# Weaving the experts of a mixture layer: products of four experts ahead of the down products of the four before

## The chip, the cores and the metric

The kernel runs on one core of a Trainium2 chip. The metric is the device time of one execution in microseconds (us). TensorE is called PE (PEld is its weight load), VectorE DVE, ScalarE ACT, GpSimd POOL, and SyncE SP. POOL and SP issue the transfers (DMAs) of this kernel's last stage.

## The reference, cut to what matters

The model is two blocks on 512 tokens of width 1024. Only the last part of the second block is touched by the change, a mixture of 32 experts in 4 groups, of which each token uses 2. In outline (the names are those of the reference or of the kernel):

```
h2 = rmsnorm(x) * (1 + scale2) + shift2            # 512 x 1024
group = argmax of 4 group logits; the 2 best of its 8 experts, with weights
for each token and each of its two experts e:
    a = silu(h2 @ w_gate[e]) * (h2 @ w_up[e])      # 256 wide
    x += gate2 * weight * (a @ w_down[e])          # 1024 wide
```

All weights are float32. An expert has 1024 x 256 for the gate, the same for up, and 256 x 1024 for down: 3 MB, so 96 MB for the 32 experts, and all of it is fetched from memory once.

## The kernel before, in words

The two blocks' dense products come first; their weights pass through `Stream`, a list of fetches in a fixed order (`order`). A fetch takes a free place of 128 x 2048 floats (1 MB) from `st.slots`, and `st.free` hands the place back when its last product is issued; `st.fill` then starts the next fetch on SP. SP issues in order, so a fetch whose place is not yet read out holds the later ones back. In the last stage there are 13 places: three of `wr`, seven of `wb` and three of `wq`.

Then comes the routing (L1840 to L2041): logits, the two best experts, a place in a table of 8 rounds x 256 rows for each token and expert (`hidx`, `r4s`). `keep_busy(n)` puts n products on PE that nobody reads. `rows_in(q)` gathers the 256 rows of round `q` from memory by two indirect DMAs on POOL into `gb[q % 2]`.

The experts are done in `NQ` = 8 rounds of four. A round fetches 12 places: 8 for gate and up (`gu`, one for each 128 of the 1024 inputs, all four experts side by side) and 4 for down (`dn`). Rows are two tiles: r = 0, in which each expert has its own 32 rows, and r = 1, whose four groups of 32 rows each belong to an expert chosen by the routing. For r = 1 `deal` copies the four 512-wide pieces of the place, chosen by registers, into `wd` (two on DVE, two on ACT; two buffers). `product` makes four 32-row products that run beside each other, and it is called once with the place itself and once with `wd`.

The order of one round is written out by hand and is the same on every engine:

- `turned` transposes and scales the gathered rows: PE products with a diagonal matrix `dg`, and 8 evictions that alternate between ACT and DVE, into `xT`;
- 8 times: `deal`, two `product`s into `bank[0]` and `bank[1]`, `st.free`, `st.fill`;
- `act` (tanh on ACT, two multiplications on DVE) for both tiles;
- `turn(q + 1, r)` for both tiles, with the gather of round q + 2 behind the second;
- `act_T` (PE transposes, ACT copies) for both tiles;
- 4 times: `deal`, two `product`s; `halves` multiplies the results into `yo` on DVE;
- two `scatter`s, indirect DMAs on POOL that add the rows of `yo` to the output in memory. Each waits for the one before it to land, as rows may repeat; only the two of the last round don't wait for each other.

`later` holds small work (`slot_weights`, the weights of the rows, and `crowded`, for experts with more rows than fit), which is stepped after a round, and `slot_weights` stands behind the first place of round 0.

Of the kernel before, what the change touches and what calls it, by code (L numbers as in the profile page):

```python
# [12 lines left out]
FT = mybir.dt.float32  # L13
# [7 lines left out]
D = 1024  # L21
# [19 lines left out]
LOTS = 32 * MAGIC  # L41
MORE0 = 7
Z1 = (1, 0, 0, 1, 2, 2, 2)
# [315 lines left out]
def tile_kernel(ctx: ExitStack, tc: tile.TileContext, ws, ada, c_d, hT_d, cst_d, seq_d, bd_d, wr_d, pos_d, out):  # L359
# [54 lines left out]
    class Stream:  # L414
# [3 lines left out]
        def __init__(self, order):  # L418
            self.order = order
            self.lp = self.sp = self.up = 0  # L420
            self.hold, self.queue = False, nc.sync
            self.raw, self.done, self.used = {}, {}, {}
            self.slots = deque(wpool.tile([128, 2048], FT, name=f"wr{i}") for i in range(self.WR))
            parts = [wpool.tile([128, 2, 1024], FR, name="wp", tag="P", bufs=self.PARTS) for _ in range(self.PARTS)]
            self.parts = deque([t[:, 0], t[:, 1]] for t in parts)

        def more(self, slots, parts):
            self.slots.extend(B([128, 2048], name="wb") for _ in range(slots))
# [47 lines left out]
        def free(self, key):  # L476
            self.slots.append(self.raw.pop(key))

# [51 lines left out]
    n_dense = [name for name, *_ in plan].index("gu")  # L530
    for n in range(len(plan)):
# [1332 lines left out]
    gb = [B([128, 2, D], name="gb") for _ in range(2)]  # L1864
    for g in gb:
        G.memset(g, 0.0)

# [54 lines left out]
    V.tensor_add(cnt_h, oh[:, 0], oh[:, 1])  # L1922
    keep_busy(2)

# [84 lines left out]

    xT = [B([128, 2, 8, 128], name="xT") for _ in range(2)]  # L2010
    wd = [B([128, 4, 512], name="wd") for _ in range(2)]
    yo = B([128, 2, D], name="yo")

# [4 lines left out]
    rows_in(0)  # L2018
    rows_in(1)
    st.hold, st.queue = False, G  # L2020
# [19 lines left out]
    V.tensor_copy(tot, pt)  # L2040
    keep_busy(6)  # L2041

    def slot_weights():

        S.activation(ex, ex, AF.Exp)
        V.reduce_sum(pg, gx, axis=AX.X)
        V.reciprocal(pg, pg)
        V.tensor_scalar(m1, ex, 1.0, None, op0=OP.add)
        V.reciprocal(m1, m1)
        V.tensor_mul(wk[:, :4], pg, m1)  # L2050
        V.tensor_mul(wk[:, 4:], wk[:, :4], ex)
# [3 lines left out]
        inv3 = bank[3][:, 32:64]  # L2055
        by_slot(inv3, ohb, lambda n: tkw[:, n].rearrange("p v a -> p (v a)"))
        values(w_s, inv3)
# [7 lines left out]
    ex_w, ex_j, hidx2 = (cpool.tile([128, NX], I32, name=n) for n in ("ex_w", "ex_j", "hidx2"))  # L2065
    r4s2, w_s2 = (cpool.tile([128, NX], FT, name=n) for n in ("r4s2", "w_s2"))

    def crowded():
# [28 lines left out]
        yield  # L2097
        inv = bank[4][:, :80]
        by_slot(inv, ohb, lambda n: tks[n // 4][:, n % 4].rearrange("p v a -> p (v a)"))
# [19 lines left out]

    def turned(x, g, scale, banks, tag="vm"):  # L2120

        d = mpool.tile([128, 128], FT, name="dg", tag=tag, bufs=1)
        V.tensor_scalar(d, ident, scale, None, op0=OP.mult)  # L2123
        for h, p in enumerate(banks):
# [16 lines left out]

    def act_T(a, p):
        for k in range(2):
            PE.transpose(p[:, 128 * k:128 * k + 128], a[:, 128 * k:128 * k + 128], ident)
        aT = mpool.tile([128, 2, 128], FT, name="aT", tag="fxpm")
        S.copy(aT, p[:, :256].rearrange("p (k s) -> p k s", k=2))
        return aT
# [4 lines left out]

    def turn(q, r):
        turned(xT[q % 2][:, r], gb[q % 2][:, r], r4s[:, 2 * q + r:2 * q + r + 1], bank[4:6] if r else bank[6:8],
               "vfm" if r else "vm")
        if r and q + 2 < NQ:
            rows_in(q + 2)
# [4 lines left out]
    dealt = [0]  # L2162

    def deal(n, regs):

        st.need(("w", n))
        w = st.raw["w", n]
        t = wd[dealt[0] % 2]
        dealt[0] += 1
        for j in range(4):  # L2170
            (V.tensor_copy if j < 2 else S.copy)(t[:, j], w[:, bass.ds(regs[j], 512)])  # L2171
        return w, t
# [7 lines left out]
    def own(w):  # L2180
        return lambda j: w[:, 512 * j:512 * j + 512]

    def done(n):
        st.free(("w", n))
        st.fill()

    st.fill()
    scatters = []
    regs = lot_regs(0)
    first = [deal(n_dense + k, regs) for k in range(2)]  # L2190
    turn(0, 0)
    for q in range(NQ):
        n0 = n_dense + 12 * q
        x = xT[q % 2]
        for k in range(8):
            w, t = first.pop(0) if first else deal(n0 + k, regs)
            for r in range(2):
                if q == k == 0 and r == 1:
                    turn(0, 1)
                product(bank[r], lambda c: x[:, r, k, c], (lambda j: t[:, j]) if r else own(w), k == 0, k == 7)  # L2200
            if q == k == 0:
                slot_weights()
                later.add(crowded())
            done(n0 + k)
        a = [act(bank[r]) for r in range(2)]
        if q + 1 < NQ:
            for r in range(2):
                turn(q + 1, r)
        aT = [act_T(a[r], bank[6 + r]) for r in range(2)]

        def halves(h):
            for r in range(2):
                V.scalar_tensor_tensor(yo[:, r, 512 * h:512 * h + 512], bank[2 + 2 * h + r], w_s[:, 2 * q + r:2 * q + r + 1],
                                       gate[h], op0=OP.mult, op1=OP.mult)

        for h in range(2):
            for k in range(2):
                n = n0 + 8 + 2 * h + k
                w, t = deal(n, regs)
                for r in range(2):  # L2220
                    product(bank[2 + 2 * h + r], lambda c: aT[r][:, k, c], (lambda j: t[:, j]) if r else own(w), k == 0, k == 1)
                done(n)
                if h and not k:
                    halves(0)
        halves(1)
        if q + 1 < NQ:
            regs = lot_regs(q + 1)
        before_q = scatters[-1:]
        scatters = [scatter(yo[:, r], hidx[:, 2 * q + r:2 * q + r + 1]) for r in range(2)]
        if q == NQ - 1:  # L2230

            tc.declare_no_dep(scatters[1].ins, scatters[0].ins, reason="no row of out in both")
            tc.add_manual_dep(scatters[1].ins, before_q[0].ins.name,
                              mybir.DependencyInfo(mybir.DependencyClass.Sync, mybir.DependencyReason.DATA),
                              reason="rows of out added to before")
        later.tick()
        later.tick()
    later.finish()
# [6 lines left out]
    with tc.For_i(0, n_any, 1) as _:  # L2245
        n_x = vload(nx_i[0:1, 0:1], NX)
        with tc.For_i(0, n_x, 1) as i:
# [10 lines left out]
            V.tensor_copy(sw[:, 1:], w_s2[:, bass.ds(i, 1)])  # L2258
            g, x, y = gb[0][:, 0], xT[0][:, 0], yo[:, 1]
            gather(g, idx)  # L2260
            turned(x, g, sw[:, :1], bank[6:8])
# [3 lines left out]
            V.memset(yo[:, 0, :1], 0.0)  # L2265
            for h in range(2):
# [31 lines left out]
```

## Time and profile before

| what | value |
|---|---|
| median of 3 runs | 1641.91 us (1639.06 to 1643.56) |
| the profiled execution, its own time | 1641.11 us |
| its span in the trace | 1639.3 us |
| PE busy, share of the span | 1532.5 us, 93% |
| DVE, ACT, POOL busy | 927.4, 659.1, 200.5 us |
| moved by DMA over the whole span | 258.28 MB, mean 158 GB/s |

The span runs from the first to the last record of the program. The rest of the profiled time, 1.8 us, lies outside it. All times of rows are counted from the span's start. The last stage begins near 1313 us, when the dense products end.

### The profile page before, as it was taken

How to read it: one execution, taken by the hardware profiler on the slowest of the kernel's cores; microseconds unless marked ns; L12 is line 12 of the kernel's file. 1: busy time of each engine (PE TensorE's matmuls, PEld its weight loads, DVE VectorE, ACT ScalarE, POOL GpSimd, SP SyncE). 2: the span in 40 equal slices, each digit the busy share in tenths (PEclk: the TensorE clock that was granted, in tenths of full speed). 3: DMA queues.
4: the chain of work that ended last, by engine and by line, in shares of the span. 5: the costliest groups of instructions: out<-in, count | busy, mean ns of one | idle time of the engine just before them, and what ended most of it. 6: DMA issues, size and time to landing. Idle time of an engine off the chain costs nothing. (4 is left out here: it accounts for less than half of the span.)

```text
span 1639.3 us, 22545 instructions
## 1 busy us (share of the span) xinstructions
PE 1532.5 (93%) x8512; PEld 1173.7 (72%) x8512; DVE 927.4 (57%) x2020; ACT 659.1 (40%) x1208; POOL 200.5 (12%) x255
## 2 busy tenths in 40 slices
PE   7899999999999899999999999999999977877785
PEld 6788777788888678888889887778887843433432
DVE  5655456355667776654445746953666355555453
ACT  4445443326533232222234446543233224544553
POOL 0100111020030300000004223100114030111101
PEclk9999999999999999999999999999999989999998
DMA  5221221122245355454222322123226648999993
GB/s 194 81 78 66 101 68 64 66 105 88 78 176 196 126 208 197 181 189 166 103 78 104 128 91 77 53 78 106 74 78 271 208 158 329 363 382 357 372 384 82
DMA packets 49327, 258.28 MB, mean 158 GB/s; under 512 B 7316, under 2 KB 15636, under 8 KB 21184
## 3 DMA queue, kind: packets, MB, share of 16 engines
q1 hardware_dynamic: 41680, 237.17, 38.2%
q0 software_dynamic: 7248, 19.65, 4.1%
q8 instruction: 67, 1.10, 0.3%
q14 instruction: 44, 0.36, 0.1%
q10 hardware_dynamic: 288, 0.01, 0.0%
HBM read 250.48 MB, written 14.71 MB: 162 GB/s over the span
## 5 line engine op out<-in xcount | busy, mean ns | idle before, releaser
L485 DVE TENSOR_TENSOR wp<-wr,wp 128x1024 fp32r<-128x1024 f32 (+1 forms) x198 | 246.1, 1246 | 198.8 <-ACT wp L484 198.1
L484 ACT CAST wp<-wr 128x1024 fp32r<-128x1024 f32 (+1 forms) x198 | 204.0, 1034 | 110.6 <-PE bank L584 82.2
L582 PE MATMUL bank<-uh,wp 128*128 128x512 f32 (+1 forms) x464 | 150.9, 361 | 5.4 <-DVE ka L789 4.4
L584 PE MATMUL bank<-ul,wp 128*128 128x512 f32 (+1 forms) x464 | 144.5, 348 | 0.0
L586 PE MATMUL bank<-uh,wp 128*128 128x512 f32 (+1 forms) x464 | 144.1, 347 | 0.0
L582 PE MATMUL bank<-fh,wp 128*128 128x512 f32 x304 | 119.4, 393 | 6.6 <-ACT wp L484 6.6
L586 PE MATMUL bank<-fh,wp 128*128 128x512 f32 x304 | 119.3, 392 | 0.6 <-DVE wp L485 0.5
L584 PE MATMUL bank<-fl,wp 128*128 128x512 f32 x304 | 119.1, 392 | 0.2 <-POOL fl L1180 0.2
L582 PE MATMUL bank<-z,wp 128*128 128x512 f32 x264 | 108.4, 411 | 0.0
L586 PE MATMUL bank<-z,wp 128*128 128x512 f32 x264 | 103.2, 391 | 0.0
L584 PE MATMUL bank<-z,wp 128*128 128x512 f32 x264 | 103.0, 390 | 0.0
L2178 PE MATMUL bank<-wd,xT 128*32 128x512 f32 x512 | 87.5, 629 | 13.0 <-DVE wd L2171 13.0
L582 PEld LDWEIGHTS bank<-uh,wp 128*128 128x128 f32 x464 | 81.0, 190 | 24.1 <-issue 6.8
L586 PEld LDWEIGHTS bank<-uh,wp 128*128 128x128 f32 x464 | 81.2, 190 | 11.2
L584 PEld LDWEIGHTS bank<-ul,wp 128*128 128x128 f32 x464 | 81.2, 190 | 9.9
L2171 ACT COPY wd<-wb 128x512 f32 x108 | 60.6, 621 | 55.3 <-PE bank L2178 38.6
L582 PE MATMUL bank<-ah,wp 128*128 128x512 f32 (+1 forms) x218 | 76.1, 349 | 0.0
L584 PE MATMUL bank<-al,wp 128*128 128x512 f32 (+1 forms) x218 | 75.9, 348 | 0.0
L586 PE MATMUL bank<-ah,wp 128*128 128x512 f32 (+1 forms) x218 | 75.9, 348 | 0.0
L582 PEld LDWEIGHTS bank<-fh,wp 128*128 128x128 f32 x304 | 57.6, 189 | 19.3 <-ACT wp L484 7.4
L2126 PE MATMUL bank<-dg,gb 128*128 128x128 f32 x256 | 38.9, 315 | 30.8 <-DVE dg L2123 30.8
L586 PEld LDWEIGHTS bank<-fh,wp 128*128 128x128 f32 x304 | 57.4, 189 | 13.5 <-DVE wp L485 1.7
(629 smaller groups left out, 3263.0 us busy)
## 6 DMA issues: line engine op xcount, KB each, us to landing
wr<-in_ws_dram SPq DMA_DIRECT2D x115, 1024.0 KB, 4.8
wb<-in_ws_dram SPq DMA_DIRECT2D x54, 1024.0 KB, 10.8
wr<-in_ada_dram SPq DMA_DIRECT2D x24, 1024.0 KB, 5.2
wq<-in_ws_dram SPq DMA_DIRECT2D x21, 1024.0 KB, 9.4
wr<-in_ws_dram SPq DMA_DIRECT2D x4, 768.0 KB, 4.2
ncb<-cum_d POOLq DMA_DIRECT2D x8, 264.0 KB, 3.8
wr<-in_ws_dram SPq DMA_DIRECT2D x4, 512.0 KB, 5.6
h_d<-row SPq DMA_DIRECT2D x8, 256.0 KB, 3.9
```

Source lines behind the costliest of these rows:

```text
L484: S.copy(h[:, :fl], t)
L485: eng.tensor_sub(l[:, :fl], t, h[:, :fl].bitcast(FT))
L582: PE.matmul(ps, lhsT=wh(k), rhs=rh(k, sl), start=first and k == 0, stop=False)
L584: PE.matmul(ps, lhsT=wh(k), rhs=rl(k, sl), start=False, stop=False)
L586: PE.matmul(ps, lhsT=wl(k), rhs=rh(k, sl), start=False, stop=last and k == nk - 1)
L2126: PE.matmul(p[:, 128 * t:128 * t + 128], lhsT=g[:, 512 * h + 128 * t:512 * h + 128 * t + 128], rhs=d, start=True, stop=True)
L2171: (V.tensor_copy if j < 2 else S.copy)(t[:, j], w[:, bass.ds(regs[j], 512)])
L2178: PE.matmul(ps[c], lhsT=x(c), rhs=w(j), start=first, stop=last)
```

## The change

The order of the fetches and of all engines' work in the expert stage is changed. The 12 places of a round are no longer worked in one piece: the list `jobs` has the 8 gate and up places of round q, then the 4 down places of round q - 1. One loop over `jobs` does `deal` for the next place, then both products of the present one. What stood between gate/up and down (`act`, `act_T`, `turn`, the gather) is put behind single places of the next round by `beside`: `act` of round q - 1 behind place 0 of round q, `act_T` behind 2, the two `turn`s of round q + 1 behind 4 and 6. Gate and up sums alternate between banks 0, 1 and banks 2, 3; down sums use banks 4 to 7.

`EARLY` = 3 further places are added before the routing, so that 16 places can be fetched ahead. When the first three of the places drawn from pool `B` are freed they are not used for fetches again: they become the second `gb` and `xT` and `yo`. So the gather of round 1 and the zeroing of its `gb` move behind place 2 of round 0. `slot_weights` moves from place 0 to place 2 of round 0, its last part to round 1. `keep_busy` gets 9, 8 and 2 products where it had 2, 5 and 6 (a fourth call keeps its 2).

```diff
-MORE0 = 7
+MORE0, EARLY = 7, 3
...
+    fours = [(q, n_dense + 12 * q) for q in range(NQ)]
+    jobs = []
+    for q, n in fours:
+        jobs += [(q, n + k) for k in range(8)]
+        if q:
+            jobs += [(q - 1, n - 4 + k) for k in range(4)]
+    jobs += [(NQ - 1, n + 8 + k) for k in range(4)]
+    order += [("w", n) for _, n in jobs]
...
         def free(self, key):
-            self.slots.append(self.raw.pop(key))
+            t = self.raw.pop(key)
+            if self.left and any(t is x for x in self.early):
+                self.left -= 1
+                self.early = [x for x in self.early if x is not t]
+            else:
+                self.slots.append(t)
...
+    st.more(EARLY, 0)
     st.fill()
     st.hold = True
...
-    keep_busy(2)
+    keep_busy(9)
...
-    keep_busy(5)
+    keep_busy(8)
...
     rows_in(0)
-    rows_in(1)
...
-    keep_busy(6)
+    keep_busy(2)
...
+    def beside(q, k):
+
+        other = bank[2 - 2 * (q % 2):4 - 2 * (q % 2)]
+        aside[0] = other[1]
+        if q and k == 0:
+            acts(q - 1)
+        elif q and k == 2:
+            acts_T(q - 1)
+        elif k in (4, 6) and q + 1 < NQ:
+            turn(q + 1, k // 2 - 2, other)
+            if k == 6 and q + 2 < NQ:
+                rows_in(q + 2)
+        if q == 0 and k == 2:
+            rows_place()
+            rows_in(1)
+            yo.append(B([128, 2, D], name="yo"))
+            later.add(slot_weights())
+        elif q == 1 and k == 3:
+            later.finish()
+            later.add(crowded())
+        elif q > 1 and k in (5, 7):
+            later.tick()
...
+    for i, (q, n) in enumerate(jobs):
+        if i + 1 < len(jobs):
+            dealt[i + 1] = deal(i + 1)
+        w, t = dealt.pop(i)
+        k = n - n_dense - 12 * q
+        for r in range(2):
...
+            product(ps, x, (lambda j: t[:, j]) if r else own(w), first, last)
+        st.free(("w", n))
+        w = t = None
+        st.fill()
+        if k < 8:
+            beside(q, k)
+        elif k == 10:
+            halves(q, 0)
+        elif k == 11:
+            halves(q, 1)
+            add_rows(q)
+            aT.pop(q)
```

## Rows read from the trace of the kernel before

**Rows 1.** Page, busy tenths of the DMA engines in 40 slices of 41 us.

```profile
DMA  5221221122245355454222322123226648999993
```

**Rows 2.** Windows, one round: us; PE, PEld, DVE, ACT, POOL busy; granted clock; DMA.

```profile
1387.00:1402.00 15.00, 14.77 (x120) 7.15 (x120) 6.04 (x17) 7.22 (x13) 1.56 (x1) 0.89 1.01 378
1402.00:1412.50 10.50, 4.65 (x39) 4.11 (x36) 4.80 (x14) 4.11 (x11) 2.09 (x2) 1.00 0.98 403
1412.50:1420.00 7.50, 7.46 (x64) 2.14 (x64) 5.19 (x12) 5.94 (x12) 0.00 (x0) 1.00 0.74 276
1420.00:1423.00 3.00, 1.00 (x9) 0.96 (x8) 2.24 (x4) 0.85 (x2) 1.62 (x1) 1.00 0.97 311
```

**Rows 3.** Timeline, the same round from its last gate and up products on.

```profile
1400.05 1.20 PE L2178 MATMUL bank<-wb,xT 128*32 128x512 f32 x8
...
1400.91 1.20 PE L2178 MATMUL bank<-wd,xT 128*32 128x512 f32 x8
...
1403.77 2.05 PE L2126 MATMUL bank<-dg,gb 128*128 128x128 f32 x16 [1.66 <-DVE dg L2123]
1404.97 0.46 ACT L2133 ACTIVATE xT<-bank,mod,a 128x128 f32<-128x128 f32 x1 [2.36 <-PE bank L2126]
...
1408.34 2.05 PE L2126 MATMUL bank<-dg,gb 128*128 128x128 f32 x16 [2.52 <-DVE dg L2123]
...
1412.54 1.06 PE L2178 MATMUL bank<-wr,aT 128*32 128x512 f32 x8 [1.71 <-ACT aT L2146]
```

**Rows 4.** DMA queues from 1380 to 1608 us: packets, MB, share of 16 engines.

```profile
DMA packets 13706, 83.47 MB, mean 366 GB/s; under 512 B 2844, under 2 KB 2844, under 8 KB 4216
...
q1 hardware_dynamic: 10666, 77.58, 84.8%
q0 software_dynamic: 3020, 5.63, 10.6%
```

**Rows 5.** Windows, columns as in rows 2: the stretch, fetches alone, after the last fetch.

```profile
1380.00:1608.00 228.00, 180.49 (x1462) 89.38 (x1458) 119.57 (x299) 114.96 (x227) 29.39 (x21) 0.94 0.96 366
...
1400.00:1410.00 10.00, 5.82 (x50) 4.20 (x43) 3.66 (x10) 2.95 (x7) 1.06 (x1) 1.00 1.01 421
...
1608.00:1610.00 2.00, 2.00 (x24) 1.05 (x20) 0.99 (x3) 1.42 (x3) 0.27 (x1) 1.00 0.03 8
```

**Rows 6.** Timeline of SP: the fetches of the last stage as they restart.

```profile
1315.14 1.67 SPq L440 DMA_DIRECT2D wq<-in_ws_dram  x3
...
1351.22 9.93 SPq L440 DMA_DIRECT2D wb<-in_ws_dram  x6
```

**Rows 7.** Timeline of PE and POOL from the routing to the third place.

```profile
1315.07 1.88 PE L1862 MATMUL bank<-mbig,ident 128*128 128x512 f32 x4
1319.97 0.62 PE L1928 MATMUL bank<-cnt,marks 128*128 128x32 f32 x4 [3.02 <-DVE cnt L1922]
...
1327.12 1.35 PE L1987 MATMUL bank<-tk,ohb 128*128 128x16 f32 x8
...
1329.60 1.14 POOL L2006 DMA_INDIRECT gb<-h_d,hidx  x1 [3.29 <-DVE tk L1982]
...
1336.17 1.95 PE L2126 MATMUL bank<-dg,gb 128*128 128x128 f32 x16
...
1349.18 1.94 PE L2178 MATMUL bank<-wb,xT 128*32 128x512 f32 x8
```

**Rows 8.** One line's instructions, the gathers L2006 from 1327 to 1339 us.

```profile
DMA to landing us min/median/max: 4.0/4.3/5.8
```

**Rows 9.** Timeline of POOL at the end: the scatters of the last two rounds.

```profile
1599.88 1.71 POOL L2150 DMA_INDIRECT out_dram<-yo,hidx  x1 [19.93 <-DVE yo L2213]
1609.73 1.67 POOL L2150 DMA_INDIRECT out_dram<-yo,hidx  x1 [8.14 <-DVE wd L2171]
1624.43 1.56 POOL L2150 DMA_INDIRECT out_dram<-yo,hidx  x1 [13.03 <-DVE yo L2213]
```

**Rows 10.** DMA issues from 1608.5 to 1615 us: count, us to landing.

```profile
out_dram<-yo,hidx POOLq DMA_INDIRECT x1, 4.6
```

More of the change, by code (lines that the diff above doesn't have):

```diff
@@ L422, in __init__ @@
             self.raw, self.done, self.used = {}, {}, {}
+            self.early, self.left = [], 0
             self.slots = deque(wpool.tile([128, 2048], FT, name=f"wr{i}") for i in range(self.WR))
@@ L427, in more @@
         def more(self, slots, parts):
-            self.slots.extend(B([128, 2048], name="wb") for _ in range(slots))
+            new = [B([128, 2048], name="wb") for _ in range(slots)]
+            self.slots.extend(new)
+            self.early.extend(new)
             for _ in range(parts):
@@ L530, in tile_kernel @@
     n_dense = [name for name, *_ in plan].index("gu")
-    for n in range(len(plan)):
+    for n in range(n_dense):
         order.append(("w", n))
@@ L1862, in keep_busy, with rows_place @@
             PE.matmul(bank[1], lhsT=ident, rhs=io, start=True, stop=True)
-    gb = [B([128, 2, D], name="gb") for _ in range(2)]
-    for g in gb:
-        G.memset(g, 0.0)
+    gb, xT, yo = [], [], []
+    def rows_place():
+        gb.append(B([128, 2, D], name="gb"))
+        G.memset(gb[-1], 0.0)
+        xT.append(B([128, 2, 8, 128], name="xT"))
+    rows_place()
     sc, used = [], [0]
@@ L2054, in slot_weights @@
         spread_a(G, tkw, tf, tok[:, :, 3:])
-        inv3 = bank[3][:, 32:64]
+        yield
+        inv3 = bank[7][:, :32]
         by_slot(inv3, ohb, lambda n: tkw[:, n].rearrange("p v a -> p (v a)"))
@@ L2117, in crowded, with norm_of, turned @@
             yield
-    def turned(x, g, scale, banks, tag="vm"):
+    def norm_of(scale, tag):
         d = mpool.tile([128, 128], FT, name="dg", tag=tag, bufs=1)
         V.tensor_scalar(d, ident, scale, None, op0=OP.mult)
+        return d
+    def turned(x, g, d, banks):
         for h, p in enumerate(banks):
@@ L2140, in act, with act_T @@
         return a
-    def act_T(a, p):
+    def act_T(a, p, aT=None):
         for k in range(2):
             PE.transpose(p[:, 128 * k:128 * k + 128], a[:, 128 * k:128 * k + 128], ident)
-        aT = mpool.tile([128, 2, 128], FT, name="aT", tag="fxpm")
+        if aT is None:
+            aT = mpool.tile([128, 2, 128], FT, name="aT", tag="fxpm")
         S.copy(aT, p[:, :256].rearrange("p (k s) -> p k s", k=2))
@@ L2151, in scatter, with turn, deal @@
                                     in_offset=None, bounds_check=SEQ - 1, oob_is_err=False, compute_op=OP.add)
[L2153 to L2157, printed above, removed]
+    def turn(q, r, banks):
+        turned(xT[q % 2][:, r], gb[q % 2][:, r], norm_of(r4s[:, 2 * q + r:2 * q + r + 1], "vfm" if r else "vm"), banks)
     def lot_regs(q):
         return [vload(lot_i[0:1, 4 * q + j:4 * q + j + 1], 1536, [ET.DVE if j < 2 else ET.Activation]) for j in range(4)]
-    dealt = [0]
-    def deal(n, regs):
+    regs, dealt = {}, {}
+    def deal(i):
+        q, n = jobs[i]
+        if n == n_dense + 12 * q:
+            regs[q] = lot_regs(q)
         st.need(("w", n))
         w = st.raw["w", n]
-        t = wd[dealt[0] % 2]
-        dealt[0] += 1
+        t = wd[i % 2]
         for j in range(4):
-            (V.tensor_copy if j < 2 else S.copy)(t[:, j], w[:, bass.ds(regs[j], 512)])
+            (V.tensor_copy if j < 2 else S.copy)(t[:, j], w[:, bass.ds(regs[q][j], 512)])
         return w, t
@@ L2181, in own @@
         return lambda j: w[:, 512 * j:512 * j + 512]
[L2183 to L2229, printed above, removed]
@@ L2230, in tile_kernel, with halves, add_rows @@
+    def halves(q, h):
+        for r in range(2):
+            V.scalar_tensor_tensor(yo[0][:, r, 512 * h:512 * h + 512], bank[4 + 2 * h + r], w_s[:, 2 * q + r:2 * q + r + 1],
+                                   gate[h], op0=OP.mult, op1=OP.mult)
+    def add_rows(q):
+        last = scatters[-1:]
+        scatters[:] = [scatter(yo[0][:, r], hidx[:, 2 * q + r:2 * q + r + 1]) for r in range(2)]
         if q == NQ - 1:
             tc.declare_no_dep(scatters[1].ins, scatters[0].ins, reason="no row of out in both")
-            tc.add_manual_dep(scatters[1].ins, before_q[0].ins.name,
+            tc.add_manual_dep(scatters[1].ins, last[0].ins.name,
@@ L2234, in tile_kernel, with acts, acts_T @@
                               mybir.DependencyInfo(mybir.DependencyClass.Sync, mybir.DependencyReason.DATA),
                               reason="rows of out added to before")
-        later.tick()
-        later.tick()
+    a, aT, scatters = {}, {}, []
+    def acts(q):
+        a[q] = [act(bank[2 * (q % 2) + r]) for r in range(2)]
+    def acts_T(q):
+        p = bank[2 * (q % 2)]
+        aT[q] = [act_T(x, p[:, 256 * r:256 * r + 256], SM([128, 2, 128], name="aT") if q == NQ - 1 else None)
+                 for r, x in enumerate(a.pop(q))]
@@ new lines, in tile_kernel @@
+    st.fill()
+    st.left = EARLY
+    turn0 = [norm_of(r4s[:, r:r + 1], "vfm" if r else "vm") for r in range(2)]
+    dealt[0] = deal(0)
+    turned(xT[0][:, 0], gb[0][:, 0], turn0[0], bank[2:4])
+    for i, (q, n) in enumerate(jobs):
[3 more added lines that the diff above has]
+        k = n - n_dense - 12 * q
+        for r in range(2):
+            if i == 0 and r == 1:
+                turned(xT[0][:, 1], gb[0][:, 1], turn0[1], bank[4:6])
+            if k < 8:
+                ps, x = bank[2 * (q % 2) + r], lambda c: xT[q % 2][:, r, k, c]
+                first, last = k == 0, k == 7
+            else:
+                ps, x = bank[4 + 2 * (k // 10) + r], lambda c: aT[q][r][:, k % 2, c]
+                first, last = k % 2 == 0, k % 2 == 1
+            product(ps, x, (lambda j: t[:, j]) if r else own(w), first, last)
+        st.free(("w", n))
+        w = t = None
+        st.fill()
+        if k < 8:
+            beside(q, k)
[5 more added lines that the diff above has]
+            aT.pop(q)
+        if q == NQ - 2 and k == 8:
+            acts(NQ - 1)
+        elif q == NQ - 2 and k == 10:
+            acts_T(NQ - 1)
@@ L2258, in tile_kernel @@
             V.tensor_copy(sw[:, 1:], w_s2[:, bass.ds(i, 1)])
-            g, x, y = gb[0][:, 0], xT[0][:, 0], yo[:, 1]
+            g, x, y = gb[0][:, 0], xT[0][:, 0], yo[0][:, 1]
             gather(g, idx)
-            turned(x, g, sw[:, :1], bank[6:8])
+            turned(x, g, norm_of(sw[:, :1], "vm"), bank[6:8])
             for k in range(8):
@@ L2264, in tile_kernel @@
             aT = act_T(act(bank[0]), bank[1])
-            V.memset(yo[:, 0, :1], 0.0)
+            V.memset(yo[0][:, 0, :1], 0.0)
             for h in range(2):
```

6 lines of the change are left out of this document (3 added, 3 removed).

## The prediction

> **What bounds the kernel now.** I read the page first. The DMA engines are idle or half busy through the dense products and then at nine tenths for the last six slices, where the experts run [rows 1]; so the question in that stage is whether the fetches or the engines set the pace. The windows over one round answer it in part. In the 15 us of the gate and up products PE is full, then it works for 4.65 of 10.5 us, is full again in the down products and has 1 of 3 us at the round's end [rows 2]. DVE and ACT add up to 18.3 and 18.1 us in these 36 us. No engine is full, yet PE waits, so the order is the limit there. The timeline shows how: PE's last gate and up product starts at 1400.91 and the first down product at 1412.54, with both `turned` between, the second of which waits for the diagonal on DVE, which stands behind the evictions of the first [rows 3]. All this time the fetches go on: from 1380 to 1608 us they take 84.8% of the DMA engines, the gathers and scatters 10.6% [rows 4]. The round is thus a loop with some 10 us of bubble, and close beneath it lies a second limit, the transfers, which has 4 to 5% left. Last, I looked at both ends: before the first round PE waits for the routing and then for `slot_weights` [rows 7]; after the last fetch, in by 1608 us [rows 5], PE still has nearly a whole round before it and the last pair of scatters starts at 1624.43 [rows 9].
>
> **What the change makes of a round.** With the weaving each place costs PE two products .86 us apart [rows 3], 1.72 us for a place and 20.6 for 12. The two `turned` take 2.05 us each, 4.1. The transposes of `act_T` have no row here; they are fewer products than one `turned`, so between nothing and 2.05, and I take 1. A `turned` also holds up the copies of the place after next: its evictions begin 1.2 us after its products and end about 3.1 us later [rows 3], and the copies stand behind them on DVE and ACT, 0.8 to 1.1 us more. PE in that time has the rest of `turned`, a place and the first product of another, 4.6 us of its own; it waits 0.5 to 0.8 us, 1.6 a round at most. Sum 27.3 us. DVE and ACT have 18.3 and 18.1 us of work in it [rows 2], so their cover holds: `act`'s multiplications and the `halves` fill the time between copies. Without that cover `act`, `turn` and `act_T` would cost the 11.6 us that they cost now.
>
> A round of transfers: a place is 1.049 MB. Fetches alone ran at 421 GB/s [rows 5], 2.49 us a place; over the whole stretch 77.58 MB took 84.8% of 228 us, 193 us, 2.61 a place [rows 4]. With a dozen places asked for ahead the queue is deep, as in the first of these rows, so I take 2.5 and keep 2.61 as the upper bound. Gathers and scatters took 10.6% of 228 us, 24.2 us for 21 (8 and 13, by the code's order), 1.15 each; a round has four. So 12 x 2.5 + 4.6 = 34.6 us. The transfers become the bound: rounds of 27 us eat up the lead of the places fetched ahead, and the second half runs at the pace of the fetches.
>
> **The start.** `keep_busy` puts two records of 0.43 us on PE for each product (the 4 of `keep_busy(2)` took 1.88 us [rows 7]; the step is that of a product above, halved). Nine are 7.7 us from 1315.07, to 1322.8, while the counts are ready at 1319.9: 2.9 us late. The eight after the counts (1.5 us) hold PE until 1331.2, where the placing products stood at 1327.12 [rows 7]: 4.1 us late. The first gather moves from 1329.6 to 1333.7, lands 4.0 to 5.8 us later [rows 8], and the first `turned` starts near 1338.5 instead of 1336.2. Should PE's clock be lower here, the delay is longer; should it be none, 2.5 us come back. Then the wait for `slot_weights` falls away: the second place starts at 1349.18 now [rows 7] and the third ends near 1349 then. The memset and the gather of round 1 wait for that on POOL, land near 1356, and PE, which meets the first `turn(1, 0)` at about 1353, waits 3 us: what was early is now late, and behind it stand the copies of the next places. I get a restart of the fetches at about 1351, as now [rows 6], then a hole of some 3 us, and unbroken fetching from 1367 us on with 76 of 96 places to come. The three further places serve here: 16 places are in before the restart, on DMA engines that were idle, rather than 13.
>
> **The end.** 76 x 2.5 = 190 us, and 23 gathers and scatters (10 and 13) x 1.15 = 26.5: the last place lands at L = 1367 + 216.5 = 1583.5. Its products take 2 us more, the last `halves` could let the scatters go at about L + 2.5. But the scatters of round 6 are now only four places, 10 us of fetching, ahead. The first of them goes at about L - 8; the second goes 9.85 us behind the first [rows 9], at L + 2, and lands 4.6 us later once fetches are over [rows 10]; only then, 0.75 us on, can the last pair go: L + 7.4. Now the last pair waits for `yo`, then it waits for a landing, 5 us. From there to the end of the span it is 1639.3 - 1624.4 = 14.9 us, unchanged. Span 1605.8; with the 1.8 us outside it 1607.6; the median lies 0.8 above the profiled execution, so **1608.5 us**, 33 us less. With 2.61 us a place it is 1617.
>
> One rule of the Trainium skill speaks against this step. The row: in the 2 us from 1608 DVE is at work for 0.99, copies as ever, the fetches are over [rows 5], and a scatter lands in 4.6 us [rows 10], against the 9.85 from one to the next under the fetches. The Trainium skill (SBUF — State Buffer, section "SBUF: two separate sides") says that DVE's float32 copies within SBUF lock POOL out of a port, so that it can't write descriptors and a DMA of POOL's seems blocked. By it the scatter would be as slow beside copies alone, and the end some 5 us later; by the row it is the fetches that slow it.
>
> **The rivals.** (1) Fetches do not get faster than now: the mean of 366 GB/s over everything [rows 4] is a ceiling, and the fetches hide what the order gains. Left after 1367 are 79.7 MB of places and 23 x 0.27 = 6.2 MB: 234.7 us, span 1367 + 234.7 + 22.3 = 1624, time 1627. For it speaks that the engines were at 96% already [rows 5]; against it, ten microseconds at 421 GB/s in one piece [rows 5]. The Trainium skill (DMA: Bandwidth & Descriptors, section "Specifications") gives about 358 GB/s as the share of memory of one core; as an estimate that would be 1632, and the 421 GB/s of the rows are above it.
>
> (2) The engines stay the bound, because the copies queue behind evictions and `act` far more than I counted. The four places of round 6 and their scatters then end at 1367 + 7 rounds, and the span 30 us later. With rounds of 33 us, 6 over my sum, the time is 1630. For it: a place's copies wait for PE and PE for the copies, in one line per engine. Against it: DVE and ACT at half load [rows 2].
>
> (3) Slower: PE waits between places for fetches, its clock falls to the lower of its two levels (1.2 GHz for 2.4), and a place takes 3.44 us. All low, a round is 41.3 + 8.2 + 1.6 = 51 us, against 27; by the formula of (2) the gain is gone from rounds of 34.6 us on, with a third of the work at the lower level; at half, 39 us, the time is 1672. For it: the granted clock is already 0.89 in a row with PE full [rows 2]. Against it: over the stretch, with bubbles of 10 us, it is 0.94 [rows 5], about an eighth of the time low, and a PE that falls behind is busy again without pause.
>
> **How the numbers follow.** The forecast, 1600 to 1618 us, has 0.57; still less, if the start isn't delayed or the scatters pass sooner, 0.07; rival (1) 0.16; rival (2), 1618 to 1636, 0.09; rival (3) 0.07; and 0.04 for no change, where a loss at the start or the end eats a rest of rival (2)'s gain. A measurement of this kernel can tell 0.3%, 5 us, from no change. So faster 0.89, same 0.04, slower 0.07. The range of 1598 to 1627 leaves out the slow ends of (2) and (3) and what lies below the forecast.
>
> **What would show it.** Right: no stretch of 10 us without products inside a round; early rounds of some 27 to 30 us and late ones near 34.6; copies and PE that wait for a fetch in the second half, as they hardly do now; fetches above 400 GB/s without the breaks; the last fetch near 1584; the last scatters waiting for the ones before. Wrong: PE waiting for copies in every round (2), a granted clock well under 0.9 (3), or DMA engines full at 366 GB/s (1). A first `turned` before 1336 would show the cost of `keep_busy` wrong.

## The result, and the profile after

The changed kernel takes 1618.5 us (median of 4 runs, 1617.3 to 1618.7) against 1641.6 for the kernel before (4 runs on the same chip): a ratio of 0.9858, with a 95% interval of 0.9841 to 0.9876. It is 23 us faster where 33 were forecast; the time lies in the range, 10 us above the point. The profiled execution has a span of 1616.7 us and a mean granted clock of 0.987 (0.978 before).

**The ends and the whole.** The page's line that answers to [rows 1], busy tenths of the DMA engines by slices of 40 us:

```profile
DMA  5221221222235255445222241222223866999992
```

Five slices stand at nine tenths, as before (the prediction read six). In the slice around the routing the engines are busier, and the two-tenths slice at the end holds the 24 us behind the last fetch. The timeline of PE and POOL from the routing on, against [rows 7]:

```profile
1315.57 7.89 PE L1880 MATMUL bank<-mbig,ident 128*128 128x512 f32 x18
1322.90 0.92 PE L1951 MATMUL bank<-cnt,marks 128*128 128x32 f32 x4
...
1331.22 1.35 PE L2010 MATMUL bank<-tk,ohb 128*128 128x16 f32 x8
...
1333.70 1.14 POOL L2029 DMA_INDIRECT gb<-h_d,hidx  x1 [4.18 <-DMA wb<-in_ws_dram]
...
1338.07 2.02 PE L2152 MATMUL bank<-dg,gb 128*128 128x128 f32 x16 [1.06 <-DMA gb<-h_d,hidx]
...
1341.52 1.80 POOL L1886 MEMSET gb<- 128x2048 f32 x1 [5.36 <-DVE xT L2157]
1343.60 1.21 POOL L2029 DMA_INDIRECT gb<-h_d,hidx  x1 [0.27 <-POOL gb L1886]
...
1351.63 2.05 PE L2152 MATMUL bank<-dg,gb 128*128 128x128 f32 x16
```

`keep_busy` delays the counts and the placing as worked out (1322.90 and 1331.22; 1322.8 and 1331.2 in the forecast). The gather of round 1 goes at 1343.6 and `turn(1, 0)` at 1351.63 waits for nothing.

**The rounds.** A round goes from the first gate and up place of one round to that of the next. The windows, columns as in [rows 2], for rounds 1 to 4 together, then 5, 6 and 7 one by one:

```profile
1361.00:1480.00 119.00, 110.44 (x933) 47.17 (x929) 74.39 (x205) 71.86 (x146) 16.31 (x12) 1.00 1.01 398
1480.00:1515.90 35.90, 30.07 (x239) 11.06 (x231) 18.25 (x46) 17.92 (x36) 5.43 (x4) 1.00 1.01 389
1515.90:1550.00 34.10, 29.34 (x228) 11.00 (x228) 16.75 (x42) 17.98 (x36) 3.52 (x2) 1.00 1.01 396
1550.00:1585.80 35.80, 29.01 (x200) 7.36 (x204) 15.71 (x39) 16.93 (x34) 3.42 (x2) 0.95 0.82 318
```

Rounds 1 to 4 take 29.75 us each with PE busy for 27.6 of them; the next three 35.5 (the first product of round 5 is at 1480.41), 34.1 and 35.8. The 10.5 us in which PE worked for 4.65 [rows 2] are gone. What the copies wait for changes at the same place. The groups of waits for a fetch, first all of them from 1367 to 1480 us, then the four largest from 1480 to 1592 us (engine, tile, line and what it waited for: us in all, times, longest):

```profile
ACT wd L2197 <- DMA wb<-in_ws_dram: 1.2, 1, 1.2
...
DVE wd L2197 <- DMA wb<-in_ws_dram: 0.7, 1, 0.7
```

```profile
ACT wd L2197 <- DMA wb<-in_ws_dram: 21.1, 16, 2.0
DVE wd L2197 <- DMA wr<-in_ws_dram: 19.6, 8, 3.8
...
DVE wd L2197 <- DMA wb<-in_ws_dram: 15.9, 13, 3.6
ACT wd L2197 <- DMA wr<-in_ws_dram: 14.8, 8, 3.2
```

So the lead of fetched places lasts until 1480 us, when 56 of 96 places have been used, and from there each place is used as it lands.

**The transfers.** The DMA view of the whole stretch, from the restart's end to the last landing (1592.4), against [rows 4]; the first line is the busy share in 40 slices of 5.6 us:

```profile
DMA  9999999999999999999999999999999999999524
...
q1 hardware_dynamic: 10799, 78.61, 85.5%
q0 software_dynamic: 3005, 5.56, 10.6%
```

Fetches take 85.5% of 225 us, 192.4 us; gathers and scatters 23.9. Their sum of 216.3 us is close to the forecast's 216.5. But the last place lands at 1592.4, 225.4 us after 1367. The rest lies in the last slices, where the share falls to a half and to a fifth while places are still to come. The same view from 1580 to 1592.4 us, slices of 0.3 us:

```profile
DMA  2222222221112111111111111111983848667672
...
q0 software_dynamic: 130, 0.32, 17.5%
q1 hardware_dynamic: 113, 0.79, 15.6%
```

Five places land in this window, at 1582.2, 1584.9, 1587.2, 1589.7 and 1592.4: still one in 2.5 us. But only 0.79 MB of fetches moves, not 5 x 1.05 MB; the rest of these places had come before. 15.6% of 16 engines is the work of two and a half. The fetches' queue in two parts of the window, 1580 to 1583 and 1585.5 to 1588.5 us:

```profile
q1 hardware_dynamic: 45, 0.32, 25.6%
```

```profile
q1 hardware_dynamic: 20, 0.15, 11.8%
```

This is four engines and then two. The trace, which holds every packet and every landing, says the same one by one. A landing is recorded in 16 steps; those of the last place come at 1576.1 (the first), 1578.6 (the eighth), 1580.6 (the twelfth), 1585.6 (the fourteenth) and twice at 1592.4. From 1585.6 on the packets of the fetches, 8 KB each, run two at a time and end to end, 0.31 us each, which is also the median from 1400 to 1570 us. So the two last engines are not slow at the end, they are behind. A place is 128 such packets, eight for each of 16 engines, and eight take 2.5 us: that is why places still land at the old pace. A place is in when the last of its engines is done.

**The end.** The timeline of POOL, against [rows 9], and the last `halves` on DVE:

```profile
1586.65 1.71 POOL L2177 DMA_INDIRECT out_dram<-yo,hidx  x1 [22.03 <-DVE yo L2211]
1595.37 1.56 POOL L2177 DMA_INDIRECT out_dram<-yo,hidx  x1 [7.01 <-DMA out_dram<-yo,hidx]
1601.79 1.55 POOL L2177 DMA_INDIRECT out_dram<-yo,hidx  x1 [4.87 <-DVE yo L2211]
```

```profile
1594.63 0.75 DVE L2211 SCALAR_TENSOR_TENSOR yo<-bank,w_s,cst 128x512 f32<-128x512 f32 x1 [1.41 <-DMA out_dram<-yo,hidx]
...
1600.10 2.07 DVE L2211 SCALAR_TENSOR_TENSOR yo<-bank,w_s,cst 128x512 f32<-128x512 f32 x3 [4.72 <-DMA out_dram<-yo,hidx]
```

The scatters of round 6 land at 1594.61 and 1600.01; the last pair goes 9.4 us after the last fetch, and the span ends 14.9 us later. The bracket on the last `halves` is a second reading: they wait for those landings too, since there is one `yo`.

### The profile page after: what moved, and what is told of

The parts are those of the page before. It is cut to its first block, busy times and chain, and to the rows that moved or that the text cites. A ratio compares the mean times of both kernels' runs of the same rounds, so it can differ in the third digit from the quotient of the medians.

```text
span 1616.7 us, 22593 instructions
## 1 busy us (share of the span) xinstructions
PE 1537.2 (95%) x8524; PEld 1153.4 (71%) x8524; DVE 923.3 (57%) x2020; ACT 657.0 (41%) x1208; POOL 201.2 (12%) x255
## 5 line engine op out<-in xcount | busy, mean ns | idle before, releaser
L2204 PE MATMUL bank<-wd,xT 128*32 128x512 f32 x512 | 78.5, 603 | 0.9 <-DVE wd L2197 0.6
L601 PEld LDWEIGHTS bank<-fl,wp 128*128 128x128 f32 x304 | 57.5, 189 | 12.8 <-POOL fl L1197 0.8
```

Source lines behind the costliest of these rows:

```text
L601: PE.matmul(ps, lhsT=wh(k), rhs=rl(k, sl), start=False, stop=False)
L2204: PE.matmul(ps[c], lhsT=x(c), rhs=w(j), start=first, stop=last)
```

## The experiments

The theory after the result: in the late rounds the fetches are the bound, and most of the 10 us missing come from DMA engines that don't end together. Its rivals: the engines' order is the bound all along; the start's delay comes through to the end; the last scatters cost it.

**Half of each place, in the changed kernel (e1) and in the kernel before (e2).**

```diff
-                self.queue.dma_start(t[:, :nu * fl], ws[n][:, :nu * fl])
+                f = nu * fl // 2 if n >= n_dense + 24 else nu * fl
+                self.queue.dma_start(t[:, :f], ws[n][:, :f])
```

> The changed kernel, with only the first half of each place fetched from the third round on (the products read what lay in the other half, so the output is not the reference's). Theory: in the changed kernel the fetches set the pace from about the fifth round on, and the engines alone need 29.7 us a round (as its rounds 1 to 4 show). Then all rounds take 29.7 us, the down places of round 6 end near 1361 + 7 x 29.7 = 1569 us, the scatters follow in 5 to 6 us each, and the time is 1595 to 1600 us. Rival: the engines set the pace in the late rounds too, and waits for fetches only take the place of others; then the time stays within 4 us of 1618.

> The kernel before with the same halving of the fetches from the third round on (the output is not the reference's). Theory: before, the hand-written order on the engines sets the pace and fetches are hidden, so halving them leaves the time at 1634 to 1643 us (a little less at most, as gathers and scatters land sooner). Rival: the fetches, at 96% of the DMA engines, were the limit before already; then the time falls by more than 15 us, below 1627.

Measured in one run each: 1590.9 us after (27.6 less) and 1642.0 before (1641.7 for the kernel before beside it). Rounds 5 and 6 of e1, from the first gate and up product of one round to that of the next, and the stretch of [rows 5] in e2:

```profile
1480.18:1509.28 29.10, 26.82 (x235) 11.95 (x231) 18.27 (x47) 17.89 (x36) 5.39 (x4) 1.00 0.80 255
1509.28:1536.70 27.42, 26.80 (x236) 11.93 (x232) 16.46 (x43) 17.88 (x36) 3.18 (x2) 1.00 0.76 246
```

```profile
1380.00:1608.00 228.00, 180.50 (x1456) 88.63 (x1452) 119.08 (x296) 114.60 (x226) 30.20 (x22) 0.93 0.65 200
```

In e2 the DMA share falls from 0.96 to 0.65, and PE's work in the 228 us stays at 180.5: before, the fetches bound nothing, though they were close. In e1 rounds 2 to 5 take 29.1 to 30.9 us, like the early ones of the changed kernel, and round 6 takes 27.4. That the fetches are the bound in the late rounds, and the engines' 27 to 31 us the next one, is shown. The time fell below the 1595 to 1600 expected, which had reckoned with 29.7 for every round: the last two are shorter, round 7 some 24 us, as no `turned` is left in it.

**No places ahead (e3).** `EARLY = 3` becomes 0.

> The changed kernel without the three further places (EARLY = 0). Theory: the three fetches then go out as the first three places are freed, from 1344 us on, and 4 to 5 us of their 7.6 us fall into time in which the DMA engines are idle anyway (they restart at 1349 us in the changed kernel); the rest moves the last landing: 2 to 5 us slower, 1620 to 1624 us. Rival one: three fetches ahead are worth their full 7.6 us, as all that follows is bound by fetches: 1626 us. Rival two: the places don't matter, the weaving alone does it: within 1 us of 1618.5.

Measured in 4 runs: 1623.4 us (1622.6 to 1624.1), ratio 0.9893 (0.9876 to 0.9910), 4.9 us more than the changed kernel. Three places of 2.5 us would be 7.5. But the first three places that come free are not used again in the changed kernel. Where they are, the fetches restart at 1344.77 (timeline of SP) and not at 1349.23, and from 1340 to 1367 us they move 6.82 MB rather than 5.28 (DMA view): 1.54 MB, 3.7 of the 7.5 us. That leaves 3.8; besides, this execution came to the stage 0.6 us later (its first fetch there at 1316.25, not 1315.64). Together they are the 4.4 us by which its span is longer. The places ahead are worth 5 us of the 23.

**The last down products later (e4).** The down products of round 6 stand behind the fourth place of round 7 rather than the eighth, so that its scatters can go earlier.

```diff
-        jobs += [(q, n + k) for k in range(8)]
+        early_dn = 4 if q == NQ - 1 else 8
+        jobs += [(q, n + k) for k in range(early_dn)]
         if q:
             jobs += [(q - 1, n - 4 + k) for k in range(4)]
+        jobs += [(q, n + k) for k in range(early_dn, 8)]
...
-        if q == NQ - 2 and k == 8:
+        if q == NQ - 1 and k == 7:
             acts(NQ - 1)
-        elif q == NQ - 2 and k == 10:
             acts_T(NQ - 1)
```

> The changed kernel with the last order altered: the four down places of round 6 stand behind the fourth place of round 7 and no longer behind the eighth. Theory: the last pair of scatters waits for the chain of the two of round 6 (it starts 9.4 us behind the last landing, where its own rows are ready 2.6 us behind it); with the chain ten microseconds earlier the last pair goes as soon as its rows are there, 6 to 7 us earlier: 1611 to 1613 us. Rival: the end of the span hangs on the last landing alone and the scatters would be served later anyway, or the products behind the eighth place of round 7, with nothing between them and the down products, give the time back: 1617 to 1620 us.

Measured in 4 runs: 1617.5 us (1616.7 to 1618.8), ratio 0.9858 (0.9841 to 0.9874); no difference. The first scatter of round 6 does go earlier, at 1577.03, and the second at 1587.99, but the last pair at 1601.05. The timeline shows one thing that took the gain:

```profile
1587.72 1.14 ACT L2199 COPY wd<-wb 128x512 f32 x2 [3.25 <-SPq L2300]
...
1588.76 0.65 ACT L2165 ACTIVATE ea<-bank 128x256 f32<-128x256 f32 x2
...
1591.87 1.94 PE L2206 MATMUL bank<-wb,aT 128*32 128x512 f32 x8
...
1600.96 0.75 DVE L2213 SCALAR_TENSOR_TENSOR yo<-bank,w_s,cst 128x512 f32<-128x512 f32 x1 [0.19 <-PE bank L2206]
1601.05 1.55 POOL L2179 DMA_INDIRECT out_dram<-yo,hidx  x1 [11.46 <-DVE yo L2213]
```

The last `act` stands on ACT behind the copies of the first down place, which wait for its fetch until 1587.7; PE, done with the gate and up products at 1585.6, has only two short transposes until the products at 1591.87, and then the last rows are late. The other thing is the last place itself: it lands at 1596.3 and not at 1592.4. Behind that landing the pair goes after 4.8 us rather than 9.4, so 4.6 us were won there and 3.9 lost before it. Both scatters of round 6 now stand ahead of the last landing; at the 1.9 us that e6 gives for one, that is 3.8 us, an estimate that no run tests by itself. The rival held: what was moved gave its gain back.

**`keep_busy` as before (e5).** 2, 5 and 6 in place of 9, 8 and 2.

> The changed kernel with the fillers for PE as before: keep_busy of 2, 5, 2 and 6 products. Theory: the fillers of the change hold the routing up by 3 to 4 us but keep the granted clock at 1.00; with the old ones the first turned starts near 1336 us instead of 1338, the granted clock falls below 0.9 somewhere before 1360 us, and the two about cancel by the restart of the fetches: 1615 to 1620 us. Rival: the fillers are a part of the gain, and without them the first places run at the lower clock for long, 1622 us or more.

Measured in 4 runs: 1617.2 us (1615.9 to 1618.0), ratio 0.9851 (0.9833 to 0.9868); no difference. The windows around the routing, first of the changed kernel, then of e5:

```profile
1313.00:1336.00 23.00, 23.00 (x95) 13.44 (x95) 11.94 (x54) 3.46 (x6) 5.61 (x10) 1.00 0.79 301
```

```profile
1313.00:1336.00 23.00, 19.98 (x90) 12.38 (x90) 13.87 (x62) 4.78 (x9) 5.76 (x10) 0.93 0.82 317
1336.00:1367.00 31.00, 30.10 (x245) 14.96 (x243) 18.04 (x50) 19.43 (x42) 9.52 (x11) 1.00 0.62 227
```

With the old fillers the first gather goes at 1331.24, 2.5 us earlier, at a mean clock of 0.93 rather than 1.00; behind it the clock is 1.00 in both. The fetches restart at 1348.9, against 1349.2, and the last lands at 1592.8, against 1592.4. But this execution of e5 began the stage 1.1 us later (first filler at 1316.71, not 1315.57). Counted from there the gather is 3.6 us earlier, the first `turned` only 1.4, as the six products of the last `keep_busy` hold PE until 1337.8, and the restart 1.5. So less than half of the delay reaches the restart, and what is left of it at the end, 0.7 us, is within the spread of the runs.

**No scatters in rounds 0 to 5 (e6), no gathers from round 3 on (e10), and fetches almost alone (e8).** e6 returns from `add_rows` for q < 6; e10 from `rows_in` for q > 2; e8 does both, and leaves out the second tile's copies and products from round 2 on.

```diff
     def add_rows(q):
+        if q < NQ - 2:
+            return
```

> The changed kernel without the scatters of rounds 0 to 5 (their rows are not added to the output). At issue is the term of 1.15 us a gather or scatter, and the last 17 us before the last landing, in which the DMA engines are on average at 0.57 and then 0.23 of the time busy though a place lands every 2.5 us. Theory one, the mean: 12 scatters less are 14 us less, L = 1578, time 1603 to 1607 us, and the idle stretch at the end stays as it is. Theory two: scatters load a few of the 16 engines more than the others, these lag, and the last landing waits for them; then the time falls by 17 us or more (to 1601 us or less, 1591 at least, where the engines' own pace sets the floor) and the stretch below 0.6 shrinks to a third.

> The changed kernel without the scatters of rounds 0 to 5, without the gathers from round 3 on, and from round 2 on without the copies and products of the second row tile (none of these results are the reference's), so that from round 2 on nothing but fetches is in the DMA queues and PE asks for less than they give. Theory one, the 16 DMA engines are uneven by themselves: with fetches alone the mean busy share again falls under 0.6 more than 10 us before the last landing. Theory two, gathers and scatters make them uneven: the share stays above 0.9 until 4 us before the last landing. In both a place lands every 2.5 to 2.6 us, the last one near 1557 to 1565 us.

> Leaves out the ten gathers of rounds 3 to 7 (these rounds work on rows that were there before); scatters stay. By their mean busy time, 23.9 us for 21 of which 15.8 went with twelve scatters, the gathers are about 0.9 us each, 9 in all. Theory one: scatters, and not gathers, make the engines uneven: the last place lands about 9 us earlier, at 1583, and the stretch before it with the DMA engines less than 0.6 busy stays some 17 us long. Theory two: each transfer of POOL's adds alike: the landing is 12 to 13 us earlier, 1580, and that stretch shrinks by a third to a half. Time 1609 or 1606.

Measured in one run each: 1595.3, 1584.4 and 1607.7 us. The last place lands at 1570.4, 1561.9 and 1582.1. The windows at the end of e6, then of e8, then of e10:

```profile
1555.00:1560.00 5.00, 4.50 (x34) 1.00 (x26) 3.08 (x10) 2.88 (x7) 0.00 (x0) 1.00 0.99 410
1560.00:1565.00 5.00, 4.10 (x38) 1.33 (x42) 3.49 (x8) 2.23 (x6) 0.84 (x1) 1.00 0.51 211
```

```profile
1381.00:1550.00 169.00, 127.12 (x892) 46.60 (x895) 65.39 (x160) 37.48 (x89) 0.00 (x0) 0.88 1.01 414
1556.00:1557.00 1.00, 0.66 (x7) 0.02 (x3) 0.45 (x1) 0.00 (x0) 0.93 (x1) 0.76 0.99 410
1557.00:1558.00 1.00, 1.00 (x8) 0.14 (x8) 0.00 (x0) 0.00 (x0) 0.69 (x1) 1.00 0.75 311
```

```profile
1565.00:1570.00 5.00, 4.57 (x36) 0.98 (x31) 2.59 (x7) 2.86 (x7) 0.00 (x0) 1.00 0.66 274
```

In e8 the share is full until 5 us before the last landing; in e6 it falls 10 us before it, in e10 and in the changed kernel some 16. The DMA queues of e6 from 1367 to 1570 us, and of e10 to 1581 us, give the mean's part:

```profile
q1 hardware_dynamic: 10885, 79.20, 94.5%
q0 software_dynamic: 1343, 2.52, 4.0%
```

```profile
q1 hardware_dynamic: 10660, 77.57, 88.3%
q0 software_dynamic: 1839, 3.41, 8.5%
```

Busy sums of fetches, gathers, scatters and the instruction queues, as shares of the stretch: 217.4 of 225.4 us in the changed kernel, so 8 us are lost to the uneven end; 208.2 of 215.1, 7 us, without the gathers; 201 of 203.4, 2.4 us, without the scatters. In e8 the places land one in 2.5 us from 1381 to the end, and by this sum nothing is lost.

The last landing is 22 us earlier in e6 and 10.3 in e10. But the executions came to the stage at different times: the fetches restart at 1349.2 in the changed kernel, at 1350.3 in e6 and at 1347.6 in e10. Counted from the restart, twelve scatters cost 23 us, of which some 16 are mean busy time (23.9 to 8.1 us in q0) and 6 the lagging engines, and ten gathers cost 8.7 us. For e6 the theory of uneven engines, at least 17 us, held, against 14 by the mean; its stretch at a low share shrank to a half and not to a third. For e10 the theory that the scatters do it held: 9 us were expected by it, and the stretch stays at 16 us.

The steps of the landings show how the lag comes about. In the changed kernel the first and the last step of a place lie 1.5 us apart for one fetched at the restart (issued at 1350.9), 3 to 4 until the first scatter at 1391.87, 12 for one issued at 1445, and 15 to 20 for all that are issued from 1453 on. In the kernel before, with as many scatters, they lie 3.1 us apart in the median from 1380 us on and 6 at most; there the fetches pause in every round [rows 2], so that the price of a transfer read from its rows could not show this. For the last place of all they lie 16.2 us apart in the changed kernel, 16.3 in e10, 11.4 in e6 and 4.4 in e8. So under unbroken fetches the scatters alone spread the engines as far as all of it does; the gathers alone spread them too, but less work is lost by it.

Which engines these are, and why they fall behind, the traces don't show. The Trainium skill (DMA: Bandwidth & Descriptors, section "Latency and other measured facts") says that two of the sixteen, 7 and 15, are usually slower, with a best guess that the descriptor rings of POOL's transfers in SBUF load the ports that serve these two. That two engines end last, and that it goes with POOL's transfers, agrees with the runs (two steps at 1592.4, 6.8 us behind the fourteenth; 8 us lost, 2.4 in e6, none in e8). That they are slower packet by packet isn't seen in the last 6 us (0.31 us, as before).

**Both ends at once (e7).** e4's order, with the copies of the first down place of round 7 behind the last `act` and `act_T`, and `keep_busy` at 5 and 6.

```diff
-        if i + 1 < len(jobs):
+        final = q == NQ - 1 and k == 7
+        if i + 1 < len(jobs) and not final:
             dealt[i + 1] = deal(i + 1)
...
+        if final:
+            acts(NQ - 1)
+            acts_T(NQ - 1)
+            dealt[i + 1] = deal(i + 1)
```

> The changed kernel with both ends altered: keep_busy of 5 and 6 products where it has 9 and 8; the down places of round 6 behind the fourth place of round 7, and the copies for the first down place of round 7 behind act and act_T. Theory: in the run with the altered last order alone, act stood behind copies that wait for a fetch and 4 of the 6.6 us came back; with the copies behind it, the last pair of scatters goes at about 1597 instead of 1601.8, and the shorter fillers let the fetches restart 3 us sooner: 1610 to 1613 us. Rival: the last landing alone sets the end, and a start 3 us sooner only lengthens the wait for round 1's gather: 1616 to 1619 us.

Measured in 5 runs: 1614.3 us (1611.6 to 1616.5), ratio 0.9832 (0.9816 to 0.9849): 4 us below the changed kernel by the medians, all of its runs below all of those, though the intervals overlap a little; above the time expected. It is the fastest version of the study that does all of the work. Its profiled execution, the slowest of the five, has the last pair at 1599.89 and the last landing at 1596.8. So the pair goes 3.1 us after the last landing, where the changed kernel needs 9.4: the copies behind `act` took away what e4 still lost there. But the last landing is 4.4 us later, as in e4, and of the 6.3 us won behind it 1.9 are left in this execution. What is left at the end is the landing itself, and it moves with the scatters that stand before it.

**A second buffer for the last rows (e9).** `halves` and the scatters of the last round use `gb[0]`, free by then, in place of `yo[0]`.

> The last round writes its scaled rows into the rows' buffer of round 6, which is free by then, rather than into the one yo that the scatters of round 6 still read. In the changed kernel three of the last four halves start at 1600.10, at the landing of a scatter (1600.01), and the last pair goes at 1601.79. Theory: the last pair waits for its own buffer and not only for the landing that its order asks for; with a buffer of its own the halves are done some 3 us after the last fetch lands, and the pair goes 0.75 us behind the landing: 1.0 us earlier against the last fetch's landing (9.4 us behind it now, 8.4 then). Time about 1617.5, which one look can't tell from 1618.5; the place against the last landing can. Rival: the pair is held by something behind the landing on POOL, and stays at 9.4 us.

Measured in one run: 1616.7 us. Its last `halves` and last pair:

```profile
1592.97 2.72 DVE L2212 SCALAR_TENSOR_TENSOR gb<-bank,w_s,cst 128x512 f32<-128x512 f32 x4
...
1600.33 1.55 POOL L2177 DMA_INDIRECT out_dram<-gb,hidx  x1 [3.86 <-issue]
```

The `halves` are done at 1595.7 and not at 1602.2, and the pair goes 0.75 us after the landing at 1599.58 and 8.1 us after the last fetch (1592.2), not 9.4. The theory held; the other wait, for the landing of the scatter before, remains.

## Why the forecast was near, and where it was off

The forecast of 1600 to 1618 us was for the mechanism that it describes, and 1618.5 lies just above it. That the time is still within the wider range, 1598 to 1627, is luck in part: the upper end was rival (1), which fell, and the 10 us missing have a cause that no part of the prediction names.

**What bounded the kernel.** That the order set the pace before, with the transfers close beneath, was right, and e2 shows it: a third less of DMA time changed nothing.

**A round of engines, 27.3 us by the sum.** 29.75 measured in rounds 1 to 4, but 27.4 in round 6 of e1. What the sum left out are the steps of `crowded` and `slot_weights` on DVE and their few products on PE: in round 6 of e1 none of them is left (nor a gather), and DVE has 16.5 us of work there against 18.3 to 19.9 in the four rounds before. In the timeline of the changed kernel the diagonal of a `turned` stands behind the copies, and these behind eight such steps (1406.5 to 1407.9).

```profile
1407.91 0.75 DVE L2197 COPY wd<-wb 128x512 f32 x2
1408.59 0.28 DVE L2145 TENSOR_SCALAR dg<-ident,r4s 128x128 f32<-128x128 f32 x1
...
1408.92 2.05 PE L2152 MATMUL bank<-dg,gb 128*128 128x128 f32 x16 [1.24 <-DVE dg L2145]
```

It cost nothing at the end, since the fetches were the bound from 1480 us on; the crossing came after 56 places rather than 48 or so. The sum without these steps was right to 0.1 us, with some luck: PE is busy for 26.8 us of round 6 where the sum has 25.7, and waits for 0.6 where it has 1.6.

**A round of transfers, 34.6 us.** 35.5, 34.1 and 35.8. The price of a place was right: 2.5 us in e8, 192.4 us of mean busy time for all. Rival (1), a ceiling of 366 GB/s, fell: 398 GB/s from 1361 to 1480 us with the gathers and scatters, and 414 in e8. The 358 GB/s that the prediction cites from the Trainium skill (DMA: Bandwidth & Descriptors, section "Specifications") are passed by the mean of each of rounds 1 to 6 (388 to 402).

**The start.** The delay by `keep_busy` was right to 0.1 us as far as the first gather, and the first `turned` came at 1338.07 (1338.5). Two of its consequences were not: POOL put the memset and the gather of round 1 at 1341.5, before `slot_weights`, so that PE didn't wait for 3 us and the fetches restart at 1349.2 rather than 1351; and less than half of the delay reaches that restart (e5). At 1367 us there were 76 places to come, as in the forecast.

**The end: the term that was too small.** "23 gathers and scatters (10 and 13) x 1.15 = 26.5" took the mean busy share of 16 engines for the time until the last place is in. As a sum of busy time it came out (216.3 us for 216.5), though by two misses that cancel: 192.4 us of fetches for 190, and 23.9 for 26.5, as two of the ten gathers were issued before 1367 (21 remained, 1.14 us each). But two engines are 7 us behind all others at the end, and L is 1592.4 instead of 1583.5. Scatters lay at the root of it: without twelve of them the end moves by 23 us, counted from the restart of the fetches, 1.9 us each, without ten gathers by 8.7, 0.9 each. This is 8.9 of the 10.9 us that the span is longer than forecast. The other 2 us are the last pair, at L + 9.4 instead of L + 7.4: the first scatter of round 6 at L - 5.7 (L - 8), since its `halves` came 4.4 us and not 2.5 behind the last down place; the second 8.7 us behind it; its landing 4.6, as said; then 1.8 rather than 0.75, for the one `yo` (e9). The tail of 14.9 us was right. The early rounds and the start don't enter.

**What spoke against it.** By the Trainium skill's rule on DVE's copies (SBUF — State Buffer, "SBUF: two separate sides") the scatter at the end would be slow beside copies alone. In the changed kernel the first scatter of round 6, at 1586.65, lands in 8.0 us beside copies and the fetches of the lagging engines, which doesn't tell the two apart; the second lands in 4.6 with copies over. In e8 a scatter, at 1556.07, takes 6.2 us beside the last fetches with few copies, and the 4.6 us of [rows 10] came with copies and no fetches. So a delay without copies is seen and one by copies alone isn't; the rule doesn't show here.

**The clock.** Rival (3) fell: 1.00, the higher level, over rounds 1 to 6, against 0.94 in [rows 5]; where PE waits for single fetches at the end there is one stretch lower (0.67 from 1570 to 1575 us), in which PE waits for the fetches anyway.

## What to carry to other kernels

A mean busy share over 16 DMA engines gives the work but not the end: when a stretch is bound by transfers, look at its last slices, and if the share falls while tiles still land at the old pace, price each small indirect transfer by what the landing does, not by its share. When an order is mended, the next bound can be close beneath, as here; work out its round beforehand, and look for what is left at the ends, where a wait for a landing, one shared buffer or a copy that waits in an engine's line cost microseconds each. Before work is moved, name what it will stand behind and what will stand behind it: in e4 `act` stood behind copies that wait for a fetch, and in e4 and e7 the last fetch came 4 us later with two scatters moved ahead of it. Before rounds are read from windows, put the windows' bounds where the rounds begin.

## What the runs showed that was not expected

- Of 16 DMA engines the first is done with the last place 16.2 us before the last two, and the fourteenth 6.8 us before them; in the last 12.4 us fetches take 15.6% of the engines' time, and five places still land, one in 2.5 us.
- Under a full queue of fetches a gather of 128 rows takes 12.6 us to land in the median (the eight issued from 1367 us on) and a scatter 10.3, against 4.3 [rows 8] and 4.6 [rows 10] without; a fetch takes 22 to 24.
- Fillers on PE kept the clock at 1.00 around the routing, against 0.93 with fewer, and behind it the clock was 1.00 in both.
